# Attention heads of a decoder kernel: the weights' low parts move from GpSimd to VectorE, and a pair's scaling queues behind the copies of transposed probabilities

## The chip, the cores and the metric

The kernel runs on one core of a Trainium2 chip. The metric is device time in microseconds (us) of one execution; lower is better. Of the kernel before, three runs are shown: 1486.8, 1493.02 and 1493.02 us, median 1493.02.

## The reference

The program is a two-layer decoder trunk on 512 tokens of width 1024, in fp32. Only layer 0's attention matters here. One input projection feeds eight heads of a block-sparse attention (MoBA) and eight heads of a latent attention (MLA); the head outputs are concatenated and go through one output projection. Cut down:

```python
h = x @ w_in                                   # c_q 256 | c_kv 128 | k_rope 32 | q_b k_b v_b 512 each
q  = rms_norm(c_q) @ w_uq                      # 8 heads x (64 + 32 rotated)
kv = rms_norm(c_kv) @ w_ukv                    # 8 heads x (64 keys + 64 values)
k  = concat(kv keys, apply_rope(k_rope) for every head)
o_mla  = softmax(causal(q k^T / sqrt(96))) v   # 8 heads
o_moba = ... softmax over selected blocks ...  # 8 heads; with 512 tokens all past blocks are selected
m = concat(o_mla, o_moba) @ w_out
x = layer_norm(ALPHA * x + m); then conv FFN, then a gated per-layer embedding; then layer 1
```

## The kernel before, in words

Large products keep fp32 accuracy by splitting each operand into a high part and a low part in TensorE's faster fp32 format and adding three products (`mm3`, L106 to L109). `split` (L73 to L78) makes the parts: the high part is a copy (by ScalarE at L75, or by another engine at L77), the low part is source minus high part (L78). `split_w` (L90 to L103) does it for a 128x512 half of a loaded weight tile `raw`; which engines it uses there stands in the list `low`. The pool `rawp` has three buffers, `wp` ten. SyncE (SP) issues the weight transfers in program order, each as soon as a `raw` buffer is free, that is, when both parts of both halves of its last user have been made.

The heads are done in pairs, 0 to 3 MoBA and 4 to 7 MLA, in a loop over p = 0 to 8 (L569 to L585) whose order on TensorE is the order of the program. Each turn of the loop does, for pair p:

- `scores`: for each of four row blocks a product of queries and keys for both heads into PSUM banks `s` (L331); VectorE scales, masks and takes the row's bound (L334), ScalarE takes the exponential and its sum (L336). The larger two row blocks come first, then the smaller two.
- `turn` of pair p-1: TensorE transposes its probabilities in five groups into banks `pt` (L358), and each group is copied out to SBUF by VectorE (L361) or ScalarE (L363).
- `weights` of pair p (L338 to L346): VectorE takes the reciprocals of the sums and scales the two larger row blocks of both heads; GpSimd scales the two smaller ones (L344), for pair 7 VectorE does them too.
- `values` of pair p-1 (L365 to L371): probabilities times values into `o`, which ScalarE and VectorE split into `ob` or `om`.

`s`, `pt`, and the banks `tr`, `ct`, `kr`, `mq` of other transposes all rotate through the same four PSUM banks (pool `pb`). Between these steps the table `between` (L548 to L561) sets other products: `c` (the low-rank columns, then their norms and a rotation of 32 columns, `rope`, at L440), `uq` (queries of MLA), `vm` (values), `wo` (half of the output projection from `ob`), `om`, `pj`. `ready(p)` makes an MLA pair's keys and queries: a product `mk` per pair whose two halves are split (L75, L78) beside a small transfer of the rotated key rows (L493), and eight transposes `mq` that are split as well.

```python
low = [V, A]                       # low part by VectorE, high part by ScalarE
low[:] = G, A                      # from the loads of the heads on: low part by GpSimd
low[:] = G, V                      # from p == 5 on: low by GpSimd, high by VectorE
low[:] = V, A                      # behind the first four loads of the feed-forward part
```

The order on VectorE, ScalarE and GpSimd is not written out: a scheduler takes it from the program.

Of the kernel before, what the change touches and what calls it, by code (L numbers as in the profile page):

```python
# [33 lines left out]
def trunk(ctx, tc, I, out):  # L34
# [33 lines left out]
    def scr(name="scr", dt=F32):  # L68
        return sp.tile([P, 512], dt, tag="scr", name=name)

    low = [V, A]

    def split(h, l, src, eng=V, hi=A):  # L73
        if hi is A:
            A.activation(h, src, AF.Copy)  # L75
        else:
            hi.tensor_copy(h, src)  # L77
        eng.tensor_tensor(l, src, h.bitcast(F32), op=OP.subtract)  # L78
# [12 lines left out]
    def split_w(raw, n=1024, gain=None, tiles=None, tag="w"):  # L91
        m = n // 2
        ws = []
        for i in range(2):
            w = (tiles or wp).tile([P, 2, 512], F32R, tag=tag, name="w")
            r = raw[:, i * m:(i + 1) * m]
            if gain is None:
                split(w[:, 0, :m], w[:, 1, :m], r, *low)
            else:
                A.activation(w[:, 0, :m], r, AF.Copy, scale=gain[i])  # L100
                V.scalar_tensor_tensor(w[:, 1, :m], r, gain[i], w[:, 0, :m].bitcast(F32),
                                       op0=OP.mult, op1=OP.subtract)
            ws.append(w)  # L103
        return ws
# [156 lines left out]
    def rope(eng, x, heads, half, cos, sin):  # L261

        tmp = scr("rope")
        n = heads * half
        t1, t2, t3, t4 = (tmp[:, i * n:(i + 1) * n].rearrange("p (h f) -> p h f", f=half) for i in range(4))
        x1, x2 = x[:, :, 0:half], x[:, :, half:2 * half]
        c, s = (y[:, None, :].to_broadcast([P, heads, half]) for y in (cos, sin))
        eng.tensor_tensor(t1, x1, c, op=OP.mult)
        eng.tensor_tensor(t2, x2, s, op=OP.mult)
        eng.tensor_tensor(t3, x2, c, op=OP.mult)  # L270
        eng.tensor_tensor(t4, x1, s, op=OP.mult)
        eng.tensor_tensor(x1, t1, t2, op=OP.subtract)
        eng.tensor_tensor(x2, t3, t4, op=OP.add)


    def attention():
        with ExitStack() as es:
# [31 lines left out]
            class Pair:  # L309
# [25 lines left out]
                                                   scale=-self.scale, scalar=3e38, accum_out=nmx[:, i:i + 1])  # L335
                            A.activation(p, p, AF.Exp, bias=nmx[:, i:i + 1], scale=-1.0, accum_out=sm[:, 0, i:i + 1])  # L336

                def weights(self, alone):  # L338
                    for nmx, sm, pi in self.soft:
                        V.reciprocal(sm[:, 1], sm[:, 0])  # L340
                        for i in range(NT):
                            p = pi[i].rearrange("p j m -> p (j m)")
                            if i < 2 and not alone:
                                G.tensor_tensor(p, p, sm[:, 1, i:i + 1].to_broadcast([P, (i + 1) * P]), op=OP.mult)  # L344
                            else:
                                V.tensor_scalar(p, p, sm[:, 1, i:i + 1], None, op0=OP.mult)  # L346

                def turn(self):

                    self.pt = {}  # L350
                    for n, parts in enumerate((((0, 0),), ((1, 0),), ((0, 1), (0, 3)), ((1, 1), (1, 3)), ((0, 2), (1, 2)))):
                        b = bank("pt")
                        pt = ptp.tile([P, 512], F32, tag="pt", name="pt")
                        at = 0
                        for x, t in parts:
                            self.pt[x, t] = pt[:, at:at + (NT - t) * P]
                            for i in range(t, NT):
                                T.transpose(b[:, at:at + P], self.soft[x][2][i][:, t], ident)  # L358
                                at += P
                        if n % 2:  # L360
                            V.tensor_copy(pt, b)  # L361
                        else:
                            A.activation(pt, b, AF.Copy)  # L363

                def values(self, oT, j):  # L365

# [45 lines left out]
            proj_b(k_of(xT), I["w_qkv"][2], 512,  # L412
                   lambda t, ps: v_evac(vb, t, ps))

            low[:] = G, A
            def moba(j, x):
                r = rows_of(x)
                return ((qk[j][r, 0], qk[j][r, 1]),), vb[:, :, 2 * j + x]
# [7 lines left out]
            def c_step(t):  # L426
                ps = acc("c", 1)
                for k in range(KT):
                    step_b(ps, (xT[0][:, k], xT[1][:, k]), L["wc"][k], t, C_COLS, k == 0, k == KT - 1)
                x = xp.tile([P, D], F32, tag="x", name="hc")  # L430
                A.activation(x[:, :C_COLS], ps[:, :C_COLS], AF.Copy)
                ss = st.tile([P, 4], F32, tag="ss", name="ss")
                junk = scr("junk")
                A.activation(junk[:, :256], x[:, :256], AF.Square, accum_out=ss[:, 0:1])
                A.activation(junk[:, 256:384], x[:, 256:384], AF.Square, accum_out=ss[:, 1:2])
                rsqrt(ss[:, 2:3], ss[:, 0:1], 1.0 / 256, RMS_EPS)
                rsqrt(ss[:, 3:4], ss[:, 1:2], 1.0 / 128, RMS_EPS)
                V.tensor_scalar(x[:, :256], x[:, :256], ss[:, 2:3], None, op0=OP.mult)
                V.tensor_scalar(x[:, 256:384], x[:, 256:384], ss[:, 3:4], None, op0=OP.mult)
                rope(V, x[:, 384:416][:, None, :], 1, 16, cos[:, t, :16], sin[:, t, :16])  # L440
                hc.append(x)

            def c_transpose(j):
# [98 lines left out]
            def ready(p):  # L542

                if p >= 4:
# [9 lines left out]
                       3: ([(pp, 0, 0, 2), (pp, 0, 0, 3)], [(ct, 0), (ct, 1), (kr_step,), (ct, 2)],  # L554
                           [(uq_load, 1), (vm, 0), (uq, 0, 0)],
                           [(uq, 0, 1), (uq, 0, 2), (uq, 0, 3), (vm, 1), (vm, 2), (ready, 4), (uq, 1, 0), (vm, 3)]),
                       4: ([(uq, 1, 1), (uq, 1, 2), (out_load, 0)], [(ready, 5)], [(uq, 1, 3)], [(pj_load, 1, c4, "c4", wp, "w")]),
                       5: ([(wo, 0, 0)], [(ready, 6)], [(wo, 0, 1), (out_load, 1)], []),
                       6: ([(wo, 0, 2)], [(ready, 7)], [(wo, 0, 3)], []),
                       7: ([(wo, 1, 0), (om_load, 0)], [(wo, 1, 1)], [(wo, 1, 2)], [(wo, 1, 3), (om_load, 1)]),  # L560
                       8: ([], [], [(om_, 0, 0, (0, 1, 2)), (om_, 0, 1, (0, 1, 2))], [])}  # L561

            def fill(p, i):
                for f, *a in between[p][i]:
                    f(*a)
# [3 lines left out]
            with tc.manual_schedule(engines={mybir.EngineType.PE}):  # L569
                for p in range(9):  # L570
                    if p == 5:
                        low[:] = G, V
                        om = big.tile([P, 2, 4, 512], F32R, tag="vo", name="om")
                    if p < 8:
                        pairs[p].scores((3, 2))
                        fill(p, 0)
                        pairs[p].scores((1, 0))
                        fill(p, 1)
                    if p:
                        pairs[p - 1].turn()  # L580
                    if p < 8:
                        pairs[p].weights(p == 7)
                    fill(p, 2)
                    if p:
                        pairs[p - 1].values(ob if p < 5 else om, (p - 1) % 4)  # L585
                    fill(p, 3)
# [32 lines left out]
    def ffn(l, xs, xT, last):  # L619
        with ExitStack() as es:  # L620
# [13 lines left out]

            f0 = 2
            ws = [load_w(I["w_up"][l, f, i]) for f in range(f0) for i in range(2)]
            low[:] = V, A
            ps = up_a(ws, xT, True)
            for f in range(f0):
                tail(f, ps[2 * f], ps[2 * f + 1])  # L640
# [446 lines left out]
```

## Time and profile before

| | |
|---|---|
| median of three runs | 1493.02 us |
| the profiled execution | 1492.96 us |
| its span (first to last instruction) | 1491.2 us |
| busy share of the span: TensorE, VectorE, ScalarE, GpSimd | 98%, 57%, 43%, 14% |
| the loop over pairs | 75.1 to 242.4 us of the span |

The profiled execution's 1492.96 us are its span and 1.8 us around it. Busy shares are averages; in the profile's forty slices TensorE stands at nine tenths or more everywhere but in the fourth slice (112 to 149 us, seven tenths) and the last. In the rows below, a line's number is that of the kernel before. The row of a stretch gives its length, then each engine's busy time and its instructions, then the granted clock of TensorE as a share of full speed.

### The profile page before, as it was taken

To read this page: it belongs to the slowest core of one execution; us is meant where nothing else is said; L and a number is where in the kernel's file an instruction comes from. 1 tells how busy PE (TensorE), PEld (TensorE's weight loads), DVE (VectorE), ACT (ScalarE), POOL (GpSimd) and SP (SyncE) were. 2 spreads that over 40 slices of the span, in tenths; PEclk is the share of its full clock that TensorE was granted. 3 is DMA by queue.
4 is the path that set the end of the run, shared out by engine and by line. 5 is a ranking of instruction groups with operands and counts; after the bars stand their busy time and mean duration, and the time that the engine had idled before them with its cause. 6 is when DMAs were issued, how large, how long until landed. Compare 5 with 4: busy or idle time off the path is not lost.

```text
span 1491.2 us, 18833 instructions
## 1 busy us (share of the span) xinstructions
PE 1466.2 (98%) x7128; PEld 1213.6 (81%) x7128; DVE 844.4 (57%) x1463; ACT 639.3 (43%) x1213; POOL 203.9 (14%) x275
## 2 busy tenths in 40 slices
PE   9997999999999999999999999999999999999998
PEld 7875777988888888889888888888888888888887
DVE  5165685655454423765586776768965454533382
ACT  5476542444434322344665455454254434422331
POOL 2526453100000000000041212123100000000000
PEclk9999999999999999999999999999999999999999
DMA  6304231333233333441433323333333233332411
GB/s 231 110 29 142 68 101 58 115 100 99 87 98 98 99 100 99 169 131 60 127 101 100 113 92 107 100 101 106 106 99 99 87 99 98 99 99 90 165 57 57
DMA packets 45259, 152.71 MB, mean 102 GB/s; under 512 B 6000, under 2 KB 6640, under 8 KB 45168
## 3 DMA queue, kind: packets, MB, share of 16 engines
q1 hardware_dynamic: 39168, 135.49, 28.7%
q10 hardware_dynamic: 6000, 16.01, 3.2%
q8 instruction: 56, 0.92, 0.3%
q14 instruction: 35, 0.29, 0.1%
HBM read 145.12 MB, written 5.31 MB: 101 GB/s over the span
## 4 chain that ended last, share of the span: by engine, by line
PE 91%; DVE 3%; issue 3%; ACT 1%; POOL 1%; ACTq 0%; POOLq 0%; DVEq 0%
PE acc L108 24%; PE acc L109 24%; PE acc L107 24%; PE pg L107 2%; PE pg L108 2%; PE pg L109 2%; PE intra L917 2%; PE xTb L138 1%; PE o L370 1%; PE s L331 1%; PE pt L358 1%; DVE pr L346 1%; PE inter L921 1%; PE state L907 1%; ACT pr L336 1%
## 5 line engine op out<-in xcount | busy, mean ns | idle before, releaser
L75 ACT ACTIVATE w<-raw 128x512 fp32r<-128x512 f32 (+1 forms) x418 | 256.8, 625 | 416.6 <-PE acc L109 370.4
L78 DVE TENSOR_TENSOR w<-raw,w 128x512 fp32r<-128x512 f32 x396 | 273.5, 699 | 253.3 <-ACT w L75 253.0
L107 PE MATMUL acc<-xTh,w 128*128 128x512 f32 (+1 forms) x976 | 363.4, 374 | 0.4 <-ACT xTh L75 0.4
L108 PE MATMUL acc<-xTl,w 128*128 128x512 f32 (+1 forms) x976 | 362.8, 372 | 0.2 <-DVE xTl L78 0.2
L109 PE MATMUL acc<-xTh,w 128*128 128x512 f32 (+1 forms) x976 | 362.8, 372 | 0.0
L108 PEld LDWEIGHTS acc<-xTl,w 128*128 128x128 f32 x976 | 183.9, 188 | 32.6 <-issue 0.7
L107 PEld LDWEIGHTS acc<-xTh,w 128*128 128x128 f32 x976 | 183.1, 188 | 32.8 <-ACT xTh L75 0.6
L109 PEld LDWEIGHTS acc<-xTh,w 128*128 128x128 f32 x976 | 183.8, 188 | 31.7
L108 PE MATMUL acc<-w,h 128*128 128x512 f32 x352 | 137.1, 390 | 0.0
L109 PE MATMUL acc<-w,h 128*128 128x512 f32 x352 | 136.8, 390 | 0.0
L107 PE MATMUL acc<-w,h 128*128 128x512 f32 x352 | 136.6, 389 | 0.0
L129 POOL TENSOR_TENSOR mv<-rs,half_neg 128x1 f32<-128x1 f32 x16 | 13.4, 842 | 751.8 <-DVE rs L128 751.8
L606 DVE SCALAR_TENSOR_TENSOR conv<-acc,cw,conv 128x511 f32<-128x511 f32 x88 | 65.7, 747 | 87.5 <-ACT conv L604 87.5
L107 PE MATMUL acc<-w,xTh 128*128 128x512 f32 x224 | 87.3, 396 | 0.0
L108 PE MATMUL acc<-w,xTh 128*128 128x512 f32 x224 | 86.9, 390 | 0.0
L109 PE MATMUL acc<-w,xTl 128*128 128x512 f32 x224 | 86.4, 392 | 0.0
L107 PEld LDWEIGHTS acc<-w,h 128*128 128x128 f32 x352 | 66.1, 188 | 13.8
L108 PEld LDWEIGHTS acc<-w,h 128*128 128x128 f32 x352 | 66.1, 188 | 13.6
L109 PEld LDWEIGHTS acc<-w,h 128*128 128x128 f32 x352 | 66.1, 188 | 13.6
L604 ACT ACTIVATE conv<-acc,cw 128x512 f32<-128x512 f32 x44 | 34.3, 780 | 83.9 <-PE acc L109 83.9
L606 DVE SCALAR_TENSOR_TENSOR cv<-acc,scw,cv 128x511 f32<-128x511 f32 (+2 forms) x72 | 53.5, 744 | 23.5 <-ACT cv L604 23.0
L630 DVE TENSOR_TENSOR conv<-conv,acc 128x512 f32<-128x512 f32 x44 | 30.2, 687 | 60.1 <-PE acc L109 57.6
(280 smaller groups left out, 2275.1 us busy)
## 6 DMA issues: line engine op xcount, KB each, us to landing
raw<-in_w_up SPq DMA_DIRECT2D x88, 512.0 KB, 3.5
raw<-in_w_down SPq DMA_DIRECT2D x44, 512.0 KB, 3.5
raw<-in_w_xbc SPq DMA_DIRECT2D x24, 512.0 KB, 3.5
raw<-in_w_ple_gate SPq DMA_DIRECT2D x16, 512.0 KB, 4.5
raw<-in_w_z SPq DMA_DIRECT2D x16, 512.0 KB, 3.6
lab<-rows ACTq DMA_DIRECT2D x16, 512.0 KB, 4.4
raw<-in_w_sout SPq DMA_DIRECT2D x16, 512.0 KB, 3.5
raw<-in_w_qkv SPq DMA_DIRECT2D x11, 512.0 KB, 4.8
```

What stands on the lines that cost most here:

```text
L75: A.activation(h, src, AF.Copy)
L78: eng.tensor_tensor(l, src, h.bitcast(F32), op=OP.subtract)
L107: T.matmul(ps, lh, rh, start=start, stop=False)
L108: T.matmul(ps, lh, rl, start=False, stop=False)
L109: T.matmul(ps, ll, rh, start=False, stop=stop)
L138: T.transpose(b[:, k * P:(k + 1) * P], src[:, (half * 4 + k) * P:(half * 4 + k + 1) * P], ident)
L331: T.matmul(b[:, :e], q[:, ts], k[:, :e], start=n == 0, stop=n == len(qk) - 1)
L336: A.activation(p, p, AF.Exp, bias=nmx[:, i:i + 1], scale=-1.0, accum_out=sm[:, 0, i:i + 1])
L604: A.activation(f, ps, AF.Identity, bias=cw[:, taps:taps + 1], scale=cw[:, taps - 1:taps])
L606: V.scalar_tensor_tensor(f[:, k:], ps[:, :S - k], cw[:, taps - 1 - k:taps - k], f[:, k:], op0=OP.mult, op1=OP.add)
L630: V.tensor_tensor(g, g, pu, op=OP.mult)
L917: T.matmul(b[:, s], E[:, h], xdt[:, s], start=True, stop=True)
```

## The change

```diff
-    low = [V, A]
-                split(w[:, 0, :m], w[:, 1, :m], r, *low)
+                split(w[:, 0, :m], w[:, 1, :m], r)
...
-                def weights(self, alone):
+                def weights(self):
...
-                            if i < 2 and not alone:
+                            if i < 2:
                                 G.tensor_tensor(p, p, sm[:, 1, i:i + 1].to_broadcast([P, (i + 1) * P]), op=OP.mult)
...
                         if n % 2:
-                            V.tensor_copy(pt, b)
+                            A.activation(pt, b, AF.Copy)
                         else:
-                            A.activation(pt, b, AF.Copy)
+                            self.last = V.tensor_copy(pt, b)
...
-            low[:] = G, A
...
-                rope(V, x[:, 384:416][:, None, :], 1, 16, cos[:, t, :16], sin[:, t, :16])
+                rope(G, x[:, 384:416][:, None, :], 1, 16, cos[:, t, :16], sin[:, t, :16])
...
-                       4: ([(uq, 1, 1), (uq, 1, 2), (out_load, 0)], [(ready, 5)], [(uq, 1, 3)], [(pj_load, 1, c4, "c4", wp, "w")]),
-                       5: ([(wo, 0, 0)], [(ready, 6)], [(wo, 0, 1), (out_load, 1)], []),
-                       6: ([(wo, 0, 2)], [(ready, 7)], [(wo, 0, 3)], []),
+                       4: ([(uq, 1, 1), (out_load, 0)], [(uq, 1, 2)], [(ready, 5), (uq, 1, 3)],
+                           [(pj_load, 1, c4, "c4", wp, "w")]),
+                       5: ([(wo, 0, 0)], [], [(ready, 6), (wo, 0, 1), (out_load, 1)], []),
+                       6: ([(wo, 0, 2)], [], [(ready, 7), (wo, 0, 3)], []),
...
-                        low[:] = G, V
...
-                    if p < 8:
-                        pairs[p].weights(p == 7)
                     fill(p, 2)
+                    if p < 8:
+                        with tc.issue_after(pairs[p - 1].last.ins) if p else ExitStack():
+                            pairs[p].weights()
...
-            low[:] = V, A
```

So the low parts of the heads' weights are made by VectorE and their high parts by ScalarE; of the five copies of a turn VectorE does the first, third and fifth, ScalarE two; the scaling of pair p comes behind the last copy of pair p-1 in VectorE's queue; GpSimd scales the two smaller row blocks for pair 7 as well; the rotation of 32 columns goes to GpSimd; and the keys and queries of pairs 5 to 7 are made behind the transposes instead of ahead of them.

The kernels' own lines differ by two or three: in the changed kernel L76 is L78 of before, L205 is L207, L329 is L331, L332 is L334, L338 is L340, L344 is L346, L356 is L358, and the copies on VectorE are L361 in both. VectorE's queue at p = 5, from the end of the smaller scores on. Before:

```order
L334 ISA v,nmx<-s,mask 128x128
L334 ISA nmx 128x1
L340 RECIPROCAL sm<-sm 128x4
L346 TENSOR_SCALAR pr<-pr,sm 128x384
L346 TENSOR_SCALAR pr<-pr,sm 128x512
L340 RECIPROCAL sm<-sm 128x4
L78 TENSOR_TENSOR mk<-mk 64x512
L361 COPY pt<-pt 128x512
L346 TENSOR_SCALAR v<-v,sm 128x384
L346 TENSOR_SCALAR v<-v,sm 128x512
L78 TENSOR_TENSOR mk<-mk 64x512
L78 TENSOR_TENSOR mq<-mq 96x512
```

and now:

```order
L332 ISA v,nmx<-s,mask 128x128
L332 ISA nmx 128x1
L361 COPY pt<-pt 128x512 x3
L338 RECIPROCAL sm<-sm 128x4 x2
L344 TENSOR_SCALAR pr<-pr,sm 128x384
L344 TENSOR_SCALAR pr<-pr,sm 128x512
L344 TENSOR_SCALAR v<-v,sm 128x384
L344 TENSOR_SCALAR v<-v,sm 128x512
L76 TENSOR_TENSOR mk<-mk 64x512 x2
L205 SCALAR_TENSOR_TENSOR x<-x,wo 128x512
L76 TENSOR_TENSOR mq<-mq 96x512 x2
```

The three copies now stand ahead of the scaling, and the low parts of the next pair's keys and queries behind it. TensorE's queue at the same place. Before:

```order
L331 MATMUL s<-mk,mq 128x256 x6
L331 MATMUL s<-mk,mq 128x128 x6
L107 MATMUL mk<-cT,w 128x512
L108 MATMUL mk<-cT,w 128x512
L109 MATMUL mk<-cT,w 128x512
L500 MATMUL mq<-cst,spare 96x128 x8
L358 MATMUL pt<-cst,pr 128x128 x20
```

and now:

```order
L329 MATMUL s<-mk,mq 128x256 x6
L329 MATMUL s<-mk,mq 128x128 x6
L356 MATMUL pt<-cst,pr 128x128 x20
L105 MATMUL mk<-cT,w 128x512
L106 MATMUL mk<-cT,w 128x512
L107 MATMUL mk<-cT,w 128x512
L497 MATMUL mq<-cst,spare 96x128 x8
```

The twenty transposes moved ahead of the keys and queries. VectorE's queue at p = 3, behind the scaling of pair 2. Before:

```order
L268 TENSOR_TENSOR rope<-hc,cos 128x16
L269 TENSOR_TENSOR rope<-hc,sin 128x16
L270 TENSOR_TENSOR rope<-hc,cos 128x16
L271 TENSOR_TENSOR rope<-hc,sin 128x16
L128 TENSOR_SCALAR rs<-ss 128x1
L272 TENSOR_TENSOR hc<-rope 128x16
L273 TENSOR_TENSOR hc<-rope 128x16
L128 TENSOR_SCALAR rs<-ss 128x1
L78 TENSOR_TENSOR ob<-o,ob 128x512
L334 ISA pr,nmx<-s,mask 128x512
```

and now:

```order
L76 TENSOR_TENSOR w<-raw,w 128x384 x4
L76 TENSOR_TENSOR w<-raw,w 128x512 x2
L126 TENSOR_SCALAR rs<-ss 128x1 x2
L435 TENSOR_SCALAR hc<-hc,ss 128x256
L76 TENSOR_TENSOR w<-raw,w 128x512
L436 TENSOR_SCALAR hc<-hc,ss 128x128
L76 TENSOR_TENSOR w<-raw,w 128x512
L332 ISA pr,nmx<-s,mask 128x512
```

Eight low parts of weights took the place of the rotation ahead of pair 3's first reduction.

## Rows read from the trace of the kernel before

**Rows 1.** Busy time by stretch: turns p = 3 to 7, p = 8, the rest.

```profile
116.10:151.50 35.40, 27.84 (x136) 20.77 (x134) 18.52 (x44) 21.36 (x47) 18.58 (x39) 0.88 0.49 157
151.50:167.50 16.00, 14.55 (x91) 11.69 (x89) 11.38 (x32) 10.88 (x28) 10.36 (x23) 0.95 0.15 44
167.50:187.40 19.90, 17.87 (x98) 13.80 (x96) 11.50 (x31) 9.02 (x24) 5.37 (x12) 0.91 0.25 73
187.40:207.60 20.20, 17.76 (x97) 13.69 (x95) 15.89 (x36) 9.02 (x24) 9.02 (x9) 0.92 0.33 95
207.60:230.00 22.40, 18.76 (x99) 14.11 (x97) 18.45 (x40) 7.16 (x20) 10.85 (x8) 0.96 0.34 108
230.00:242.40 12.40, 12.40 (x68) 9.42 (x67) 5.42 (x8) 2.40 (x4) 5.38 (x4) 0.94 0.26 86
242.40:1491.20 1248.80, 1244.01 (x5996) 1038.82 (x5996) 711.53 (x1118) 511.03 (x911) 101.28 (x93) 1.00 0.32 101
```

**Rows 2.** Waits of TensorE between 75.1 and 242.4 us: total us, times, longest.

```profile
PE o L370 <- DVE pt L361: 3.6, 1, 3.6
PE pt L358 <- DVE pt L361: 3.1, 3, 1.2
PE mq L500 <- POOL spare L273: 2.9, 2, 1.5
...
PE pt L358 <- ACT cg L448: 2.3, 1, 2.3
```

**Rows 3.** Timeline of VectorE, then ScalarE, p = 5: start, length, instruction, idle before.

```profile
175.78 1.41 DVE L346 TENSOR_SCALAR pr<-pr,sm 128x384 f32<-128x384 f32 x2
...
177.21 0.65 DVE L78 TENSOR_TENSOR mk<-mk 64x512 fp32r<-64x512 f32 x1
177.78 0.67 DVE L361 COPY pt<-pt 128x512 f32<-128x512 f32 x1
178.38 0.80 DVE L346 TENSOR_SCALAR v<-v,sm 128x384 f32<-128x384 f32 x2
...
185.18 0.69 DVE L207 SCALAR_TENSOR_TENSOR x<-x,wo 128x512 f32<-128x512 f32 x1 [3.35 <-PE wo L109]
...
177.89 0.59 ACT L75 ACTIVATE mk<-mk 64x512 fp32r<-64x512 f32 x1 [0.85 <-DVE mk L78]
```

**Rows 4.** TensorE at full clock: `mk` with `mq`, `wo`; in the chain `pt`, `o`.

```profile
174.10:175.75 1.65, 1.65 (x13) 1.46 (x13) 0.87 (x7) 1.65 (x8) 0.00 (x0) 1.00 0.00 0
...
167.50:174.00 6.50, 2.90 (x12) 1.00 0.56 179
...
233.78 2.19 PE pt L358 x20
240.07 2.31 PE o L370 x16
```

**Rows 5.** Timeline of VectorE, then GpSimd, p = 7.

```profile
215.53 2.77 DVE L77 CAST w<-raw 128x512 fp32r<-128x512 f32 x2
...
226.10 1.28 DVE L361 COPY pt<-pt 128x512 f32<-128x512 f32 x2
...
215.29 8.24 POOL L78 TENSOR_TENSOR w<-raw,w 128x512 fp32r<-128x512 f32 x6 [1.53 <-ACT pr L336]
```

**Rows 6.** Timeline of VectorE: the first rotation instruction in p = 1 and p = 3.

```profile
89.30 0.18 DVE L268 TENSOR_TENSOR rope<-hc,cos 128x16 f32<-128x16 f32 x1 [0.92 <-ACT hc L431]
...
114.49 1.00 DVE L268 TENSOR_TENSOR rope<-hc,cos 128x16 f32<-128x16 f32 x1 [2.41 <-ACT hc L431]
```

**Rows 7.** Timeline of GpSimd, p = 3: a low part among the rotations.

```profile
142.48 1.28 POOL L78 TENSOR_TENSOR w<-raw,w 128x512 fp32r<-128x512 f32 x1
```

**Rows 8.** Groups by form, 75 to 262 us: low parts on VectorE, then GpSimd.

```profile
L78 DVE TENSOR_TENSOR w<-raw,w 128x512 fp32r<-128x512 f32 x2 | 1.4, 692 | 1.9 <-ACT w L75 1.9
...
L78 POOL TENSOR_TENSOR w<-raw,w 128x512 fp32r<-128x512 f32 x27 | 36.4, 1367 | 39.1 <-DVE w L77 35.6 <-ACT w L75 1.9 <-ACT pr L336 1.5
```

**Rows 9.** Transfers of the output projection's weights: KB each, median us to landing.

```profile
raw<-in_w_out SPq DMA_DIRECT2D x8, 512.0 KB, 3.6
```

More of the change, by code (lines that the diff above doesn't have):

```diff
@@ L580, in attention @@
                         pairs[p - 1].turn()
+                    fill(p, 2)
                     if p < 8:
-                        pairs[p].weights(p == 7)
-                    fill(p, 2)
+                        with tc.issue_after(pairs[p - 1].last.ins) if p else ExitStack():
+                            pairs[p].weights()
                     if p:
```

## The prediction

> **What bounds the kernel now.** I read the page first (TensorE fills the span), then busy time by stretch, since an average over 1491 us hides where TensorE stops. Behind the loop over pairs it is busy for 1244.0 of 1248.8 us at full clock [rows 1]: nothing that VectorE or GpSimd do there can be worth anything, and the change can only act in the loop. There the reader is to see two losses per turn: length less busy time, which is 7.6 us at p = 3, then 1.4, 2.0, 2.4, 3.6 and 0.0 at p = 8 (17.1 in all), and length times the missing part of the clock, 4.2, 0.8, 1.8, 1.6, 0.9, 0.7 (10.0, some of it inside the waits) [rows 1]. So at most some 25 us are to be had.
>
> Then the waits of TensorE: in turn on the copies of transposed probabilities by VectorE (3.6 before `values` at p = 7, 3.1 in three waits between groups of transposes), on GpSimd's rotation before `mq` (2.9) and on ScalarE (2.3) [rows 2]. Last the timelines, for what stands ahead of the late instruction. At p = 5 it is the scaling of the other pair: 1.41 us directly ahead of a low part and the first copy, 0.80 more ahead of the next [rows 3]. At p = 7 it is casts that take 1.39 each while GpSimd makes low parts for 8.24 us; both copies come only at 226.1 [rows 5].
>
> **The change, part by part.** The sum is made against the profiled execution, 1492.96 us; the median of the three runs, 1493.02, is the same within 0.1. Two long instructions that follow each other on VectorE start 0.61 apart (1.28 for two against 0.67 for one) [rows 3, 5].
>
> *Order of a turn, p = 5 and 6.* Now the twenty transposes follow the smaller scores, with no `mq` taking two of the four banks between, and VectorE's next work is their copies. The fifth group needs the bank of the first; three groups of 0.44 (2.19 / 5) [rows 4] lie between, and the first copy takes 0.67 [rows 3]. I expect no wait: 2.0 and 2.4 us are gained [rows 1]. The clock was short in these turns behind these waits; with none I take it at full speed: 1.8 and 1.6. So 3.8 and 4.0; the ends are the waits alone and the whole.
>
> What is late next is the following pair's keys and queries, which now stand behind the scaling. From the end of the transposes VectorE and ScalarE need: 0.45 for the start and two reciprocals (my estimate, they are the shortest instructions there), third copy 0.61, scaling 1.41 + 0.80, low part of the first key 0.6, then ScalarE's high part of the second key 0.59, which the trace shows waiting for that low part, then low part of the second key, the residual behind `wo`, first query, 0.61 each: 6.3 us [rows 3]. TensorE has `mk` and `mq` 1.65, `wo` 2.90, `values` 2.31 [rows 4] and two of the three score products, 0.5, before it needs the query's low part: 7.4. The margin is 1.0, so I cost it at nothing; if VectorE is later by more, that shows one to one.
>
> *The same at p = 4.* Its waits are 1.4 and the clock costs 0.8 [rows 1]. But there a low part of the embedding input and two of weights stand between the keys' low parts (3 x 0.61, hiding ScalarE's 0.59), and TensorE has `uq` in the place of `wo` (six products of three quarters the width: 2.90 x 6/12 x 3/4 = 1.1): VectorE 6.3 - 0.61 for the residual + 1.83 - 0.59 = 6.9, TensorE 1.65 + 1.1 + 2.31 + 0.5 = 5.6. A new wait of some 1.2 is left. Gain 1.0; ends 0 and 2.2.
>
> *Casts and GpSimd's low parts, p = 7 and 8.* High parts go to ScalarE (7.16 busy of 22.4), low parts to VectorE at 0.69 against 1.37 on GpSimd [rows 1, 8]. VectorE loses casts of 1.39 and gains low parts that start 0.61 apart. The wait of 3.6 before `values` goes, but one low part stands ahead of the first copy, which I cost at 0.6 in the transposes: 3.6 + 0.9 - 0.6 = 3.9; ends 1.5 and 4.5. At p = 8 the clock's 0.7 comes back less 0.3 of the same kind: 0.5 (rounded up); ends -1.0 and 0.7.
>
> *p = 3.* Ahead of pair 3's first reduction the rotation's four instructions go. They took 1.0 us and more beside GpSimd's low parts, 0.18 without [rows 6]. In their place come eight low parts, 4.9 (8 x 0.61), against over 4 for the rotation; the last two wait for weights of the output projection, whose transfer starts when the first two of the eight have freed a raw buffer and lands 3.6 later [rows 9]. So the reduction is hardly earlier: I take 0.5. Behind it the scaling (2.2) leaves the way of the low parts that `vm` waits for: another 0.5. On GpSimd two low parts of 1.28 leave the rotations that `mq` waits for: 2.5 [rows 2, 7]. The clock, short by 4.2 in this turn [rows 1], I take to give back 1.5, since the wait of 2.3 for ScalarE stays. Together 5.0; ends 1.0 and 7.6, the whole of the waits.
>
> *Everything else.* The turns 0 to 2 are taken as nothing. The low parts made before pair 0 lie on VectorE under a TensorE that does not wait. Scaling pair 7's two smaller blocks on GpSimd lies under `wo`, far ahead of turn 8. The four other copies changed hands between engines of which neither is full. If VectorE's cover were gone (it is busy for 11 to 18 of 20 us in turns 5 to 7, casts and all [rows 1]), the reductions would be late, and with them the banks.
>
> The sum: 5.0 + 1.0 + 3.8 + 4.0 + 3.9 + 0.5 = 18.2 us, which gives 1474.8. All low ends together, 1.0 + 0 + 2.0 + 2.4 + 1.5 - 1.0 = 5.9, give 1487.1; all high ends, 7.6 + 2.2 + 3.8 + 4.0 + 4.5 + 0.7 = 22.8, give 1470.2.
>
> **A rule against it.** The traces show that VectorE and GpSimd hold each other up: 1.00 against 0.18 for one rotation instruction with two inputs in SBUF [rows 6]. The Trainium skill, SBUF — State Buffer, section "Who interferes with whom", says that a VectorE instruction with two SBUF inputs contends with a GpSimd instruction that reads SBUF, and that the one that starts second blocks. By that rule the moved low parts, with two SBUF inputs, would be held up wherever GpSimd still works; this is rival C.
>
> **The rivals.**
>
> A. *The waits go, the clock does not come back.* For: p = 8 has no wait at all and still a clock of 0.94 [rows 1]; against: it begins behind the wait of 3.6. Then 3.5 + 0.2 + 2.0 + 2.4 + 3.0 - 0.3 = 10.8: 1482.2.
>
> B. *The scaling makes the next pair's queries late.* For: the margin is 1.0 only, and the scaling is the term that GpSimd can lengthen. If VectorE is 2 us behind the chain above, p = 4 loses 2.0 and p = 5 and 6 lose 1.0 each, with the clock's 0.8, 1.8 and 1.6 behind them: 8.2 less, 1483.0. It decides from a lateness of 1.0 on.
>
> C. *VectorE's low parts are held up by GpSimd.* Each by 0.82 (1.00 - 0.18) [rows 6]: eight ahead of the reduction at p = 3 and three at p = 4 make 9.0: 1483.8. Against: what GpSimd still does there are short rotations and its part of the scaling.
>
> D. *It does not do what it says.* Only the order of copies changes and the transposes wait as long for banks, since four banks remain four: 1493. Against: the copies at p = 5 were seen standing behind the scaling [rows 3].
>
> E. *Slower: VectorE's queue stands at transfers.* A weight's low part waits for its high part, this for a transfer, and the reductions of scores stand behind it; the transfer waits for the raw buffer that a low part frees. Where that closes into a circle, each transfer costs its 3.6 [rows 9]: one at p = 3, three over p = 6 and 7, two at p = 8, 21.6 us, and in each of four turns the clock loses 1.7 (the mean of p = 5 and 6 now), 6.8: 28.4 - 18.2 = 10.2 slower, 1503.2. It decides from the point at which the six cost over 18.2 together, 3.0 each. Against: VectorE's low part frees a buffer sooner than GpSimd's did (0.69 against 1.37) [rows 8], and none of TensorE's waits shown ends with a transfer [rows 2].
>
> **How the numbers follow.** The forecast 0.52, A 0.17, B 0.13, C 0.06, D 0.07, E 0.05. The time is that of the forecast, 1474.8. The range reaches from the high ends, 1470, to the low ends, 1487, and holds A, B and C; D and E are left out, and something for errors in a sum of many small terms. About 0.5% (7.5 us) is what a measurement of this kernel can tell from no change. Faster by more: the forecast, A, B and C, 0.88, less 0.06 for B or C coming together with A: 0.82. Within it: D and these 0.06, 0.13. Slower: E, 0.05.
>
> **What would show it.** Right: turns 5 and 6 some 16 us long, with no wait of TensorE for copies and a clock near 1.00; `values` at p = 7 without its wait of 3.6; `mq` at p = 3 waiting about 1 us or less; a wait of about 1 us at the first scores of p = 5 for a query's low part; VectorE's scaling still about 2.2. Wrong: waits of `s` on `mq` or `mk` at p = 5 to 7 (B), low parts of weights well over 0.7 (C), reductions late behind transfers (E), clocks of 0.92 without waits (A). Should the time behind the loop change in length, the argument that only the loop counts is wrong.

## The result, and the profile after

| | before | changed |
|---|---|---|
| median of four runs | 1490.47 us (1486.8 to 1493.02) | **1474.07 us** (1473.89 to 1475.73) |
| ratio | | 0.9894, 95% interval 0.9867 to 0.9922 |
| the profiled execution, its span | 1492.96, 1491.2 us | 1475.73, 1473.9 us |

The prediction was 1474.8 us (1470 to 1487), faster. By the medians the change gave 16.4 us; between the profiled executions, by which the turns below are counted, the span fell by 17.3. Busy time by stretch of the changed kernel, turns p = 3 to 8 and the rest (length, then TensorE, its weight loads, VectorE, ScalarE and GpSimd busy, then the granted clock):

```profile
114.44:146.37 31.93, 26.32 (x135) 18.43 (x134) 18.42 (x42) 20.56 (x46) 12.28 (x33) 0.95 0.48 168
146.37:159.57 13.20, 13.20 (x90) 11.15 (x88) 10.42 (x30) 10.85 (x29) 9.43 (x23) 1.00 0.15 46
159.57:176.71 17.14, 15.90 (x97) 12.57 (x95) 14.26 (x36) 9.29 (x25) 4.67 (x10) 1.00 0.30 91
176.71:192.31 15.60, 15.60 (x97) 12.65 (x95) 12.81 (x33) 9.10 (x25) 2.55 (x4) 1.00 0.22 67
192.31:212.89 20.58, 18.66 (x99) 14.69 (x97) 18.28 (x43) 12.44 (x31) 3.06 (x4) 0.92 0.50 161
212.89:225.60 12.71, 12.71 (x70) 9.13 (x70) 5.77 (x9) 4.33 (x7) 0.00 (x0) 1.00 0.26 84
225.60:1473.90 1248.30, 1243.34 (x5993) 1038.28 (x5993) 710.92 (x1118) 510.89 (x911) 102.12 (x93) 1.00 0.32 101
```

These answer to [rows 1]. Turns 4 and 6 have no wait left (length and busy time are equal) and a full clock; turn 7 has both a wait and a clock of 0.92. Behind the loop 1248.80 became 1248.30, so the change acted in the loop alone, as the prediction had it. TensorE's waits in the loop (total, times, longest), answering to [rows 2]:

```profile
PE pt L356 <- ACT cg L445: 2.5, 2, 2.2
PE pt L356 <- DVE pt L361: 1.9, 1, 1.9
PE mq L497 <- POOL spare L271: 1.5, 2, 1.2
PE vm L105 <- ACT cT L73: 0.9, 1, 0.9
...
PE s L329 <- DVE mq L76: 0.7, 1, 0.7
PE vm L107 <- DVE cT L76: 0.6, 1, 0.6
PE s L329 <- ACT mq L73: 0.5, 1, 0.5
```

Gone are the 3.6 before `values` at p = 7 and the waits for copies in turns 4 to 6; left are one of 1.9 at p = 7, the rotation's (2.9 became 1.5), ScalarE's `cg`, two before `vm` (0.7 became 1.5), and two new ones, 1.2 together, at the first scores of p = 5.

Where the 17.3 us came from, turn by turn, beside the prediction's terms (the two waits at the start of p = 5 are booked to p = 4, as the prediction did; the sum is of unrounded numbers):

| turn | 0 to 2 | 3 | 4 | 5 | 6 | 7 | 8 and behind | sum |
|---|---|---|---|---|---|---|---|---|
| predicted | 0 | 5.0 | 1.0 | 3.8 | 4.0 | 3.9 | 0.5 | 18.2 |
| measured | 1.7 | 3.5 | 1.5 | 4.0 | 4.7 | 1.8 | 0.2 | 17.3 |

VectorE at p = 6, beside p = 5 of before in [rows 3] (start, length, instruction, idle time before it):

```profile
184.05 0.69 DVE L361 COPY pt<-pt 128x512 f32<-128x512 f32 x1
184.92 0.69 DVE L361 COPY pt<-pt 128x512 f32<-128x512 f32 x1 [0.18 <-PE pt L356]
185.80 0.69 DVE L361 COPY pt<-pt 128x512 f32<-128x512 f32 x1 [0.18 <-PE pt L356]
186.40 0.23 DVE L338 RECIPROCAL sm<-sm 128x4 f32<-128x4 f32 x2
186.61 2.19 DVE L344 TENSOR_SCALAR pr<-pr,sm 128x384 f32<-128x384 f32 x4
188.72 1.10 DVE L76 TENSOR_TENSOR w<-raw,w 128x512 fp32r<-128x512 f32 x1
```

The copies come as fast as TensorE makes the transposes, and the scaling takes the 2.2 us expected of it. What the order was to do, it does. Whether it earned the gain is another question, and the runs answer it differently than the prediction did.

### The profile page after: what moved, and what is told of

Read it like the earlier page. It is cut to its first block, busy times and chain, and to the rows that moved or that the text cites. A ratio compares the mean times of both kernels' runs of the same rounds, so it can differ in the third digit from the quotient of the medians.

```text
span 1473.9 us, 18843 instructions
## 1 busy us (share of the span) xinstructions
PE 1458.1 (99%) x7128; PEld 1207.7 (82%) x7128; DVE 851.6 (58%) x1465; ACT 644.9 (44%) x1225; POOL 165.3 (11%) x261
## 4 chain that ended last, share of the span: by engine, by line
PE 93%; issue 3%; DVE 2%; ACT 1%; POOL 1%; DMA 1%; ACTq 0%; DVEq 0%; POOLq 0%
PE acc L106 24%; PE acc L107 24%; PE acc L105 24%; PE pg L106 2%; PE pg L105 2%; PE pg L107 2%; PE intra L914 2%; PE s L329 1%; PE xTb L136 1%; PE pt L356 1%; PE o L368 1%; PE inter L918 1%; PE state L904 1%; DVE w L76 1%; PE om L105 1%
## 5 line engine op out<-in xcount | busy, mean ns | idle before, releaser
L76 DVE TENSOR_TENSOR w<-raw,w 128x512 fp32r<-128x512 f32 (+1 forms) x438 | 300.9, 698 | 274.4 <-ACT w L73 273.9
L73 ACT ACTIVATE w<-raw 128x512 fp32r<-128x512 f32 (+1 forms) x438 | 268.4, 626 | 419.4 <-PE acc L107 371.2
```

## The experiments

**Theory:** the gain has two causes, the larger being the order of a turn (copies ahead of scaling, keys and queries behind the transposes), the smaller the low parts' move off GpSimd. **Rivals:** the engines of the weights' parts are all of it; the order is all of it. The first experiments undo or do one part; later ones complete a chain from the kernel before to the changed one, each step with one edit more. In kernels built on the one before, line numbers are those of before.

### Low parts alone

The kernel before without its three switches of `low`: weights' high parts on ScalarE, low parts on VectorE, throughout.

```diff
-            low[:] = G, A
-                        low[:] = G, V
-            low[:] = V, A
```

> The kernel before with one part of the change alone: every low part of a weight is made by VectorE and its high part by ScalarE; copies, scaling, rotation and the place of keys and queries stay as before. Theory (two causes, the order of a turn the larger): VectorE no longer slows down beside GpSimd, the rotation's wait at p=1 goes (1.1), the transposes of queries wait less at p=3 (1.5) and the low parts at p=7 come sooner (2 to 4), but the transposes of p=4 to 6 still stand behind scaling: about 1484 us, a gain of 5 to 8 against the kernel before. Rival 1 (the engine of the low parts is all): 1474. Rival 2 (the order is all): 1490, no gain.

Measured: 1476.92 us (1476.35 to 1477.99), ratio 0.9909 (0.9894 to 0.9924). This part alone gives 14 of the 16 us. The expected 1484 was wrong, and nearer the first rival.

### Order alone

The changed kernel with the weights' parts on the engines of before.

```diff
+            low[:] = G, A
+                        low[:] = G, V
+            low[:] = V, A
```

> The changed kernel with the weights' low parts back on GpSimd as before (from p=5 on with VectorE making the high parts); the order of copies and scaling, the place of keys and queries and the rotation on GpSimd stay changed. Theory: the gain of p=4 to 6 stays for the most part (10 of the 17 us that the change gave), the gain at p=3 and p=7 goes (5), and the rotation on GpSimd behind low parts may cost up to 2 at p=0 to 2: about 1481 us. Rival 1 (the engine of the low parts is all): 1490. Rival 2 (the order is all): 1474.

Measured: 1483.42 us (1482.99 to 1485.11), 0.9954 (0.994 to 0.9968), 2.4 above what was expected. The two parts alone are worth 14.0 and 7.5 us (1490.92 less each), together 21.5, more than the whole: they take away some of the same waits. Turns 5 and 6 are as short as in the changed kernel (16.7 and 15.6 us), but from p = 7 on it takes 1286.7 us (span 1481.3 less the start of p = 7 at 194.6), 3.1 more than before. VectorE, then GpSimd, there:

```profile
192.22 4.07 DVE L77 CAST w<-raw 128x512 fp32r<-128x512 f32 x4
196.32 0.69 DVE L78 TENSOR_TENSOR mk<-mk 64x512 fp32r<-64x512 f32 x1
...
193.21 5.42 POOL L78 TENSOR_TENSOR w<-raw,w 128x512 fp32r<-128x512 f32 x4 [0.37 <-DVE w L77]
```

Four casts of 1.0 each beside GpSimd's low parts stand ahead of the second key's low part, and TensorE waits 3.0 us for the query behind it; later 2.5 for a copy. The new order by itself thus makes the next pair's queries late, as in the prediction's rival B, but with casts in the way and not the scaling alone.

### High parts alone

The kernel before with one line out, so that weights' high parts stay on ScalarE from p = 5 on; low parts stay on GpSimd.

```diff
-                        low[:] = G, V
```

> The kernel before with the high parts of weights on ScalarE in all turns, instead of VectorE from p=5 on; the low parts stay on GpSimd. Theory: about half of what moving the low parts gave (14 us) came from VectorE's casts of 0.9 to 1.4 us beside GpSimd's low parts at p=6 and p=7, ahead of copies and queries, the other half from GpSimd's own low parts at p=1 to 4: 1483 to 1486. Rival (the casts are all of it): 1477. Rival (GpSimd's low parts are all of it, wherever the high parts are made): 1489 to 1491.

Measured: 1480.18 us (1479.92 to 1484.9), 0.9939 (0.992 to 0.9958), faster than the theory had it. So 10.2 us go with the casts, 3.3 more with the low parts' own move. But not all of the 10.2 is casts. Turn 5 is untouched by this edit (no cast stands in it), and yet it took 18.3 instead of 19.9 us. TensorE there, first before, then with the high parts moved:

```profile
177.10 0.66 PE L358 MATMUL pt<-cst,pr 128*128 128x128 f32 x4 [0.31 <-ACT pt L363]
178.51 0.66 PE L358 MATMUL pt<-cst,pr 128*128 128x128 f32 x4 [0.76 <-DVE pt L361]
180.13 0.90 PE L358 MATMUL pt<-cst,pr 128*128 128x128 f32 x4 [0.96 <-ACT pt L363]
...
181.26 0.63 PE L108 MATMUL wo<-w,ob 128*128 128x512 f32 x1
```

```profile
173.26 0.66 PE L358 MATMUL pt<-cst,pr 128*128 128x128 f32 x4 [0.31 <-ACT pt L363]
174.68 0.66 PE L358 MATMUL pt<-cst,pr 128*128 128x128 f32 x4 [0.76 <-DVE pt L361]
176.29 0.66 PE L358 MATMUL pt<-cst,pr 128*128 128x128 f32 x4 [0.96 <-ACT pt L363]
...
177.01 0.39 PE L108 MATMUL wo<-w,ob 128*128 128x512 f32 x1
```

The same three waits, to the hundredth. Behind them TensorE ran at its lower level in the one (0.63 for a product) and at the higher in the other (0.39): 1.5 us of turn 5, and 2.5 of turn 3 (35.4 against 32.9, where before has no cast either), are for the most part clock and not the edit (TensorE's busy time fell by 1.6 and 1.8 there). The median includes such luck; the runs of this kernel lie 5 us apart.

### The rest of the chain: copies, keys and queries

To the low parts alone is added, first, the new dealing of the copies:

```diff
                         if n % 2:
-                            V.tensor_copy(pt, b)
+                            A.activation(pt, b, AF.Copy)
                         else:
-                            A.activation(pt, b, AF.Copy)
+                            V.tensor_copy(pt, b)
```

> The kernel before with the low parts on VectorE throughout (1476.9 in its own run) and the copies of a turn dealt as in the changed kernel: VectorE the first, third and fifth, ScalarE two. Theory (the copies alone don't help while keys and queries stand ahead of the transposes, because their parts take banks and both engines): 1475 to 1478, no more than 2 us from the low parts alone. Rival (which engine copies first is what the transposes wait for): 1472, all of the remaining gain.

Measured: 1479.12 us (1478.32 to 1479.32), 0.9915 (0.990 to 0.993): 2.2 slower, no overlap of the runs, a little above the range expected. Then, besides it, the new places of `ready(5)` to `ready(7)`:

```diff
-                       5: ([(wo, 0, 0)], [(ready, 6)], [(wo, 0, 1), (out_load, 1)], []),
+                       5: ([(wo, 0, 0)], [], [(ready, 6), (wo, 0, 1), (out_load, 1)], []),
```

> As the kernel with low parts and copies changed, and the keys and queries of pairs 5 to 7 behind the transposes as well. What it then lacks of the changed kernel is the scaling's place behind the copies, the rotation on GpSimd and the smaller blocks of pair 7 on GpSimd. Theory: turns 4 to 6 have no wait of TensorE, as in the changed kernel without the scaling's place: 1471 to 1473. Rival (rotation or pair 7 matter): 1475 or more, with a wait at p=1 or at p=7.

Measured: 1472.30 us (1471.93 to 1473.19), 0.9871 (0.9857 to 0.9886), as expected: 6.8 us for keys and queries behind the transposes. The whole edit alone, undone in the changed kernel, shows less of it; there the copies stand ahead of the scaling anyhow, and TensorE's waits for copies in the loop come to 3.7 us, against 6.0 in the kernel with low parts and copies changed:

```diff
-                       5: ([(wo, 0, 0)], [], [(ready, 6), (wo, 0, 1), (out_load, 1)], []),
+                       5: ([(wo, 0, 0)], [(ready, 6)], [(wo, 0, 1), (out_load, 1)], []),
```

> The changed kernel with the keys and queries of pairs 5 to 7 made ahead of the transposes again. Theory: the low parts of queries then stand ahead of the copies on VectorE (1.3 for two) and hold back the transposes about 1 us in each of three turns, while the wait of 1.25 us for queries at the first scores of p=5 goes: about 1476 us, 0 to 3 slower than the changed kernel. Rival (their place is worth as much as the scaling's): 4 us a turn, 1484. Rival (only the wait at p=5 matters): 1473.

Measured: 1476.38 us (1474.49 to 1476.47), 0.9902 (0.9884 to 0.9919), as the theory had it: 2.3 slower than the changed kernel, with waits of 0.35 to 0.7 for copies in turns 4 to 6, 1.3 at p = 7, and none for queries.

### The scaling's place

```diff
-                    fill(p, 2)
                     if p < 8:
-                        with tc.issue_after(pairs[p - 1].last.ins) if p else ExitStack():
-                            pairs[p].weights()
+                        pairs[p].weights()
+                    fill(p, 2)
```

> The changed kernel with the scaling of a pair not queued behind the copies of the pair before and traced ahead of the other products, as it was before. Theory: scaling of 1.1 to 2.2 us and a reciprocal stand ahead of the copies, the transposes wait 2 to 3 us in each of p=4 to 6, with half clock behind some of these waits: 1482 to 1485 us. Rival (with the low parts on VectorE undisturbed the scaling fits in): 1474 to 1476.

Measured: 1471.53 us (1470.99 to 1471.98), 0.9872 (0.9855 to 0.9889). The theory falls, and the time lies below the rival's too: without the scaling's place behind the copies the kernel is 2.5 us **faster**. The intervals of the two ratios overlap, but the runs don't. The profiled spans differ by 4.7 us (the changed kernel's profiled execution was the slowest of its four): 1.2 over turns 4 and 5, and 3.5 from p = 7 on (1278.1 against 1281.6). VectorE of this kernel at p = 5:

```profile
167.19 0.69 DVE L361 COPY pt<-pt 128x512 f32<-128x512 f32 x1
167.93 0.18 DVE L338 RECIPROCAL sm<-sm 128x4 f32<-128x4 f32 x1
168.06 0.69 DVE L361 COPY pt<-pt 128x512 f32<-128x512 f32 x1
168.67 1.16 DVE L344 TENSOR_SCALAR pr<-pr,sm 128x384 f32<-128x384 f32 x2
169.75 0.17 DVE L338 RECIPROCAL sm<-sm 128x4 f32<-128x4 f32 x1
169.84 0.66 DVE L361 COPY pt<-pt 128x512 f32<-128x512 f32 x1
170.42 1.16 DVE L344 TENSOR_SCALAR v<-v,sm 128x384 f32<-128x384 f32 x2
```

Left free, the scheduler lets the first two copies go first by itself and puts half of the scaling between the second and the third. The third copy is 0.9 later than it could be and nobody waits for it (behind its transposes TensorE has `mk`, `mq` and `wo` to do); the keys' low parts come sooner, and the queries wait of p = 5 is gone. Turns 4 to 6 take 13.2, 15.9 and 15.6 us.

### Turn 7

In the changed kernel, turn 7: VectorE, then ScalarE, then TensorE.

```profile
201.24 2.50 DVE L76 TENSOR_TENSOR w<-raw,w 128x512 fp32r<-128x512 f32 x4 [1.27 <-ACT w L73]
203.66 0.68 DVE L205 SCALAR_TENSOR_TENSOR x<-x,wo 128x512 f32<-128x512 f32 x1
204.25 0.68 DVE L76 TENSOR_TENSOR w<-raw,w 128x512 fp32r<-128x512 f32 x1
204.86 0.68 DVE L361 COPY pt<-pt 128x512 f32<-128x512 f32 x1
...
200.58 3.23 ACT L73 ACTIVATE w<-raw 128x512 fp32r<-128x512 f32 x6 [1.45 <-DMA raw<-in_w_up]
...
205.59 0.66 PE L356 MATMUL pt<-cst,pr 128*128 128x128 f32 x4 [1.93 <-DVE pt L361]
206.01 0.68 PE L105 MATMUL wo<-w,ob 128*128 128x512 f32 x1
```

ScalarE's high parts waited 1.45 for a transfer, VectorE's low parts for them, and five low parts stood ahead of the first copy, where one had been predicted. Behind the wait of 1.9 TensorE fell to its lower level (0.63 to 0.68 for a product): `wo` took 4.6 instead of 2.9 us. (The other three runs of the changed kernel, 1.7 us shorter, may have been without this spell; they have no trace.)

The number of low parts is the smaller half of it: one more is 0.6 us, while VectorE stood idle for 1.27 ahead of them. With the scaling left free, four low parts and a residual stand ahead of the first copy too, and the transposes don't wait. VectorE, then TensorE of that kernel:

```profile
198.60 2.50 DVE L76 TENSOR_TENSOR w<-raw,w 128x512 fp32r<-128x512 f32 x4
...
200.51 2.50 PE L356 MATMUL pt<-cst,pr 128*128 128x128 f32 x20
```

There no high part was held up. In the changed kernel SyncE could issue the transfer that ScalarE waits for only when VectorE had made the low part that frees its buffer, and it landed 4.4 us later. VectorE, then SyncE:

```profile
195.41 0.68 DVE L76 TENSOR_TENSOR w<-raw,w 128x512 fp32r<-128x512 f32 x1
...
196.12 0.33 SPq L82 DMA_DIRECT2D raw<-in_w_up  x1
```

That is 3.8 us into the turn; with the scaling left free it is 3.1 us (194.14, the turn starting at 191.06), behind four low parts in a row.

To test the cause, these weights' parts were queued behind pair 6's copies on both engines (`om_load(1)` in the same way; `hold[0]()` opens two order edges as the scaling's, to the last copy on each engine):

```diff
-            ws = [load_w(I["w_up"][l, f, i]) for f in range(f0) for i in range(2)]
+            with hold[0]() if l == 0 else ExitStack():
+                ws = [load_w(I["w_up"][l, f, i]) for f in range(f0) for i in range(2)]
```

> The changed kernel with the weights loaded during p=7 (second half of the output projection for the MLA heads, first four of the feed-forward part) split behind the copies of pair 6's probabilities, on VectorE and ScalarE both; the scaling stays behind the copies. Theory: what p=7 lost (a wait of 1.9 us and then half clock for 4.6 us) comes from four low parts that stood ahead of the first copy, behind high parts that waited for a transfer: without them p=7 and all behind it take 1278.1 us instead of 1281.6, as in the kernel without the scaling's place: 1470.5 to 1471. The wait for queries at p=5 stays. Rival (the first copy was late for another reason, its bank or the reductions): 1474. Rival (the feed-forward part's weights come late): 1475 or more.

Measured: 1475.65 us (1474.99 to 1477.64), 0.9902 (0.9884 to 0.992). That these low parts made the wait at p = 7 is confirmed, the gain is not, and the time is that of the last rival: the wait at p = 7 is gone, from its scores to its values' end it took 16.8 us instead of 20.6, but what follows took 1266.5 us instead of 1261.0 in the profiled execution (the slowest of its six), since the same stands one turn later. ScalarE, then TensorE:

```profile
212.45 1.15 ACT L73 ACTIVATE w<-raw 128x512 fp32r<-128x512 f32 x2 [2.36 <-DMA raw<-in_w_up]
214.84 1.15 ACT L73 ACTIVATE w<-raw 128x512 fp32r<-128x512 f32 x2 [1.24 <-DMA raw<-in_w_up]
215.90 0.58 ACT L361 ACTIVATE pt<-pt 128x512 f32<-128x512 f32 x1
...
216.53 0.57 PE L358 MATMUL pt<-cst,pr 128*128 128x128 f32 x2 [2.39 <-ACT pt L361]
```

High parts that wait for a transfer now stand ahead of ScalarE's copy of pair 7, TensorE waits 2.4 us, and a spell at the lower level follows (0.63 for a product from 217.8 to 219.9). The edit moved the wait and did not remove it.

### What is left: turn 3

The kernel with the scaling left free (1471.5) still waits 3.3 us for `cg` at p = 3. ScalarE there stands 1.9 us at issuing two stores. They were moved to SyncE:

```diff
-        nc.scalar.dma_start(done[l, half][:, t:t + y.shape[1]], y)
+        nc.sync.dma_start(done[l, half][:, t:t + y.shape[1]], y)
```

> The changed kernel without the scaling's place behind the copies (1471.5), and the stores of the embedding's products issued by SyncE instead of ScalarE. Theory: at p=3 ScalarE stands 1.89 us at two of these issues ahead of the exponentials and of cg, for which the transposes wait 3.3 us; with the issues gone cg comes 1.5 earlier and the wait falls to about 1.8: 1469.5 to 1470.5. Rival (the issues only fill idle time of ScalarE, which then waits for something else): 1471.5. Rival (SyncE's queue is held up and weights come later): 1473 or more.

Measured: 1470.96 us (1470.37 to 1471.52), 0.9861 (0.9847 to 0.9876). The longest wait for `cg` fell to 1.7, as expected, but two shorter ones came (2.4 for the three), those for `cT` grew from 0.5 to 1.6, and turn 3 kept its length (31.6 and 31.5 us). Not to be told from 1471.5. Then the low-rank transposes went behind pair 2's:

```diff
-                       3: (..., [(ct, 0), (ct, 1), (kr_step,), (ct, 2)],
-                           [(uq_load, 1), (vm, 0), (uq, 0, 0)],
+                       3: (..., [],
+                           [(ct, 0), (ct, 1), (kr_step,), (ct, 2), (uq_load, 1)],
```

> The changed kernel without the scaling's place behind the copies (1471.5), with the transposes of the low-rank columns at p=3 behind the transposes of pair 2's probabilities and ahead of its values instead of ahead of both. Theory: the transposes of probabilities no longer wait 3.3 us for cg on ScalarE and don't run 4.8 us at half clock; vm and uq stand behind values, which cover the parts of cT for 2.4 us: a new wait of 1 to 2 us is left there; 1467 to 1469. Rival (the wait only moves to vm and uq): 1471 to 1473.

Measured: 1470.42 us (1470.34 to 1470.52), 0.9858 (0.9841 to 0.9874), between the theory's range and the rival's. Turn 3 took 29.5 us in the profile, 2.1 less; the medians show 1.1. A wait of 2.4 is left, now of the second low-rank transpose for ScalarE's copies. With both edits:

> The changed kernel without the scaling's place, with the transposes of the low-rank columns behind those of pair 2's probabilities (1470.4 by itself) and the stores of the embedding's products issued by SyncE (1471.0 by itself). Theory: ScalarE's exponentials and its copies then come 1.8 us earlier, and the wait of 2.4 us of the second low-rank transpose falls below 1: 1468.5 to 1469. Rival (that wait is set by the exponentials' own length): 1470.4.

Measured: **1470.06 us** (1468.62 to 1470.74), 0.9863 (0.9842 to 0.9883). That wait is 1.5 instead of below 1, and another of 0.9 came; against 1470.4, the rival's time, the difference can't be measured. Of the kernels run it has the lowest median, and beats both the one before and the changed one (whose fastest run took 1473.89). Last, `vm`'s last step ahead of the keys of pair 4, and the hold of turn 7's weights:

```diff
-... (vm, 1), (vm, 2), (ready, 4), (uq, 1, 0), (vm, 3)]
+... (vm, 1), (vm, 2), (vm, 3), (ready, 4), (uq, 1, 0)]
```

> The kernel just described, and besides it the weights of p=7 split behind the copies of pair 6, and the last step of vm ahead of the keys and queries of pair 4 (so that TensorE covers 0.86 us of GpSimd's rotation). Theory: the wait for copies at p=7 (0.6) goes and the wait for the rotation at p=3 falls from 1.2 to 0.4: about 1 us less than the kernel just described, 1467.5. Rival (the first scores of p=4 then wait for the query's low part by as much): the same as that kernel, within 0.5.

Measured: 1470.94 us (1470.68 to 1472.24), 0.9872 (0.9851 to 0.9892). Turn 3 is the shortest of all, 28.1 us at full clock, though the wait for the rotation stayed (1.6); a wait of 2.0 at p = 8 is new, as in the hold's own run. The `vm` edit without the hold was not run.

## Why the prediction was right, and where its steps were not

The chain of medians, each row with one edit more; the ratios' intervals are with the runs above:

| edit | us | step |
|---|---|---|
| before (three sets of runs) | 1490.4 to 1491.0 | |
| high parts of weights on ScalarE from p = 5 on | 1480.2 | -10.2 |
| low parts on VectorE | 1476.9 | -3.3 |
| copies dealt anew | 1479.1 | +2.2 |
| keys and queries behind the transposes | 1472.3 | -6.8 |
| rotation and pair 7's smaller blocks on GpSimd | 1471.5 | -0.8 |
| scaling queued behind the copies (the changed kernel) | 1474.1 | +2.5 |

A step holds all that follows from an edit, the scheduler's new order on the other engines included, and the rows come from different sets of runs. The -0.8 can't be told from nothing: the runs of the two kernels touch (1471.93 and 1471.98) and their ratios are 0.9871 and 0.9872.

Lengths of the turns, from the start of a pair's larger scores to that of the next, and from p = 7 to the end of the span:

| kernel | p=3 | p=4 | p=5 | p=6 | p=7 to end |
|---|---|---|---|---|---|
| before | 35.4 | 15.9 | 19.9 | 20.3 | 1283.6 |
| high parts moved | 32.9 | 15.3 | 18.3 | 17.4 | 1278.8 |
| low parts moved too | 30.5 | 15.2 | 17.8 | 17.0 | 1279.5 |
| copies dealt anew | 31.9 | 15.5 | 17.7 | 17.4 | 1279.4 |
| keys and queries behind | 31.9 | 13.2 | 16.1 | 15.6 | 1278.9 |
| rotation and pair 7's blocks moved, scaling left free | 31.6 | 13.2 | 15.9 | 15.6 | 1278.1 |
| the changed kernel | 31.9 | 13.8 | 16.6 | 15.6 | 1281.6 |

In each heading below stand the gain predicted and the gain measured.

**Turns 5 and 6: the size right (3.8 and 4.0; 4.0 and 4.7), the cause half wrong.** The step "order of a turn" credited the order with the waits and the whole clock. By the table the parts' engines alone bring turns 5 and 6 down by 2.0 and 3.3, of which 1.6 and 1.8 are busy time of TensorE, that is clock; the order takes what is left, and there it is the place of the keys and queries, not the scaling's, that does it. The size came out because waits and missing clock together were a bound that both causes share, and that is luck as far as the order goes: with the parts' engines alone the clock was full again with 0.4 of the 2.0 us of waits gone at p = 5 and 1.5 of 2.4 at p = 6, and in one kernel at p = 5 with none of them gone. The margin of 1.0 held at p = 6 and 7: no wait of scores there.

**Turn 4** (1.0; 1.5): no wait for copies, and the new wait predicted at 1.2 is there at 1.25, 0.5 of it for ScalarE's high part of the query. The clock gave 1.3 us of busy time, where 0.8 was taken.

**Turn 7** (3.9; 1.8) is the term that was mis-sized most. The wait before `values` went; "one low part stands ahead of the first copy" failed: five did, held up by a transfer that had waited for a buffer, and the 0.6 became 1.9 and a spell at the lower clock. That is rival E's mechanism in one place, at 1.45 us of waiting instead of 3.6: the argument against it, that none of TensorE's waits ended with a transfer, spoke of a kernel whose low parts stood on GpSimd, with no copy behind them.

**Turn 3** (5.0; 3.5). Of the four parts: the rotation's wait gave 1.4 instead of 2.5, of which VectorE's low parts, which hold up GpSimd there, make 0.9 (below); `vm` did not gain 0.5 but lost 0.8 (it waited 0.7 for a low part, now 0.9 for a high part and 0.6 for a low part); the reduction's wait of 1.2 went whole, where 0.5 was taken; and the clock gave the 1.5 it was taken to give (TensorE's busy time fell from 27.8 to 26.3 us; the granted clock rose from 0.88 to 0.95, part of it inside the waits). `cg` stayed, as predicted.

**Turns 0 to 2** (0; 1.7). At p = 1 the row quoted for the rotation's 0.18 also shows the 0.92 for which VectorE stood waiting for its input [rows 6], with a reduction queued behind it. That wait of TensorE (1.1) went, and could be read from the same row. But not by the rotation's move alone: with only the low parts moved, and the rotation still on VectorE, it is gone too. The other 0.6 lie ahead of the loop, which starts anywhere from 74.3 to 75.6 us in the kernels run.

**The sum.** Turns 3, 7 and 8 fell short by 3.9 us together, the others gave 3.1 more than was taken. That 18.2 met 17.3 is in part luck of the sum; and the sum was made against an execution near the slow end of the runs of the kernel before (1486.6 to 1493.35 us).

**Rivals.** A fell: the clock came back wherever waits went. C fell as stated: low parts take 717 ns on VectorE up to 262 us (29 of them), against 692 and 1367 [rows 8]. B's mechanism is real where its price wasn't: the scaling's place costs 2.5 us in all, mostly at the first scores of p = 5 and at p = 7. D fell with the chain.

## What to carry to other kernels

Forcing an instruction behind others to protect a wait that another edit has already removed costs whatever it then delays: try the removal first, and leave the scheduler its freedom. When a gain is read as "waits and the clock behind them", two different edits can each bring it, so only a chain of single edits tells which one did. An engine that copies for the engine that sets the end should have nothing ahead of it that waits for a transfer, and moving such work back only moved the wait here; whether transfers that start earlier would remove it was not run.

## What the runs showed of the hardware

VectorE and GpSimd hold each other up in both directions. At p = 3 of the changed kernel two low parts on VectorE took 1.64 instead of 1.28, and two rotation instructions on GpSimd beside them 0.79 and 0.77 instead of 0.32; at p = 4 one took 1.86 and VectorE lost nothing (1.28 for two). VectorE, then GpSimd, at either place:

```profile
139.66 1.64 DVE L76 TENSOR_TENSOR w<-raw,w 128x512 fp32r<-128x512 f32 x2 [2.13 <-ACT w L73]
...
139.96 0.79 POOL L269 TENSOR_TENSOR rope<-spare,sin 128x64 f32<-128x64 f32 x1
140.71 0.77 POOL L270 TENSOR_TENSOR spare<-rope 128x64 f32<-128x64 f32 x1
141.44 0.32 POOL L271 TENSOR_TENSOR spare<-rope 128x64 f32<-128x64 f32 x1
...
158.79 1.28 DVE L76 TENSOR_TENSOR w<-raw,w 128x512 fp32r<-128x512 f32 x2
...
158.40 1.86 POOL L266 TENSOR_TENSOR rope<-spare,cos 128x64 f32<-128x64 f32 x1 [0.25 <-ACT spare L467]
```

So the 0.9 us that the rotations lost lie on GpSimd, the engine that the change was to relieve; with the low parts alone moved, the rows show the same (0.77 and 0.77). The Trainium skill, SBUF — State Buffer, section "Who interferes with whom", has a VectorE instruction with two SBUF inputs contend with GpSimd's reads; the rows agree. The scaling, with one tensor input in SBUF, shows it too: two instructions of it took 0.80 us by themselves [rows 3] and from 0.96 to 1.41 with GpSimd's part of the scaling beside them, and the rows don't tell what decides between these values.

Identical waits of TensorE were followed by its lower clock in one execution and not in another (turn 5, above). The kernel before shows it at large: its runs lie between 1486.6 us, with a mean granted clock of 0.997, and 1493.35, with 0.993, and 0.004 of 1490 is 6.0 us. With few waits left, the five kernels with medians below 1471.6 spread by 0.2 to 2.1 us.

The two stores that ScalarE issues at p = 3 took 0.33 and 0.35 us of its queue in the kernel before, and 1.9 together with the scaling left free, where one of them took 1.41; taking them away was worth nothing that can be measured.
